# Tying the later modulation's fp32 matmuls together and recording them behind attention scores, in a planned one-core backbone kernel

## The chip, the cores and the metric

The kernel runs on one core of a Trainium2 chip. Its time is that of one execution on the device, in microseconds, the median of several runs. The core has TensorE (PE, the matrix engine; its weight loads are listed apart as PEld), VectorE (DVE), ScalarE (ACT), GpSimd (POOL), and SyncE (SP), whose queue issues most of the transfers between the device's memory and the core's. Every engine carries out its instructions in the order in which the program gives them to it and waits on the others by semaphores.

## The reference

Two layers over 512 latent tokens and 256 context tokens of width 1024, all in fp32. Each layer scales and shifts its normalised input by a modulation computed from a conditioning vector, mixes tokens by attention, gates, projects, and adds the result back. Layer 0 is differential attention with 8 heads, each with two maps of head dimension 64; layer 1 has 8 query heads of dimension 128 on 2 key/value heads.

```python
def adaln(cvec, w, b):
    m = jax.nn.silu(cvec) @ w + b                      # 1024 -> 3 * 1024
    return jnp.split(m, 3, axis=-1)                    # shift, scale, gate

for i in range(DEPTH):
    last = i == DEPTH - 1
    shift, scale, gate = adaln(c, ada_w[i], ada_b[i])
    cshift, cscale, cgate = adaln(c_ctx, ada_w[i], ada_b[i])
    h  = rms_norm(x,  pre_g[i]) * (1.0 + scale)  + shift
    hc = rms_norm(xc, pre_g[i]) * (1.0 + cscale) + cshift
    # layer 0: o1 - lam * o2 of two softmax maps, per-head norm, silu gate, w_out
    # layer 1: grouped queries with normalised q and k, silu gate, w_out
    y, yc = mixer(h, hc, ...)
    x = x + gate * rms_norm(y, post_g[i])
    if not last:
        xc = xc + cgate * rms_norm(yc, post_g[i])
```

## The kernel before

Weights and activations are split into a high and a low fp32r part, and a product is three matmuls (`whi` with `h` high and low, `wlo` with `h`). Projections, scores and the product of probabilities with values (PV) all run on TensorE. In layer 0 a head has six query tiles of 128: four latent ones and two of the context. Its scores (`sc<-qk,qk`) contract over 64 rows, two maps side by side in the two halves of the array: twelve matmuls for a latent query tile, or eighteen where a context tile goes with it. VectorE and ScalarE turn them into probabilities (`sm`, `p`, `pp`), a pair of query tiles shares one `pp`; VectorE transposes it in blocks of 32, SyncE writes it to memory (`dr<-pp`) and reads it back transposed (`at<-dr`, four pieces), ScalarE and VectorE split it into `ah` and `al`, and only then can TensorE do the PV matmuls (`bk<-ah,vhi` and so on).

**The later modulation.** The modulation that the start does not need (layer 0's gate and all of layer 1's, six sections named in `SECS`) is computed during layer 0's heads, in twelve groups, two for a section. `grp_load` reads 1 MB of fp32 weights (`araw`, one buffer). `grp_mm` does four fp32 matmuls of 32 columns of the array each, 512 wide, into the four quarters of one PSUM bank (`bk<-araw,s`); ScalarE copies the first group's bank to `arow`, VectorE adds the second's to it, and the next load starts. `ada1_finish` or `gate0_finish` then turns a section's row into columns (a VectorE transposition, a matmul with `fold`, small VectorE operations).

**What sets the order.** The kernel is first recorded, not built: class `Plan` keeps every operation with its producers, and a list scheduler (`schedule`) walks through it with a price for each operation. For TensorE it has four kinds: M (ordinary matmul), T (transposition), S (scores), A (32-column groups), with extra nanoseconds where the kind changes. It runs twelve passes, keeps the best, and then applies `MOVES`, a list of random seeds each of which shifts the keys of some operations (`shift`). The resulting order of each engine is fixed by `Emit.chain`, and the program is built in it. Ahead of that, `flow` decides in which sequence things are recorded: streams of `Step`s with due times, for layer 0 the scores (`S_`), the splitting of probabilities (`T_`), PV (`M_`), the per-head norm (`X_`) and the modulation groups (`A_`), between which projections of later heads and the output projection are filled in. A step may have a `HOT0` priority; `chained(prev)` makes a matmul follow `prev` with nothing between on TensorE.

In the kernel before, `acc_steps` makes each group and each finish a `Step` of its own in `A_`, without priority; `ACCN` spreads three of them over each of heads 2 to 7. All instructions carry the line of the helper that emits them (501 before, 493 after), so the profile is read by tile names: `araw` is a group, `sc<-qk` are layer 0's scores, `sc<-kh,qh` layer 1's, `raw` a weight load, `whi`/`wlo` its parts.

Of the kernel before, what the change touches and what calls it, by code (L numbers as in the profile page):

```python
# [9 lines left out]
F32 = mybir.dt.float32  # L10
F32R = mybir.dt.float32r
AF = mybir.ActivationFunctionType
ALU = mybir.AluOpType
# [3 lines left out]
P = 128  # L17
# [19 lines left out]
ACCN = (0, 0, 3, 3, 3, 3, 3, 3)  # L37
ACD = 5.0
SUMS = ()
# [50 lines left out]
CTX_AT = {2: 0, 3: 1}  # L90
DRB = 6
# [3 lines left out]
def f32(ap):  # L95
# [6 lines left out]
MOVES = (361629762, 413672696, 596582793, 497724196, 683463327, 110464215, 110999015, 165414765, 369530505, 1059228683,  # L102
# [13 lines left out]
SLACK = 0  # L116


# [22 lines left out]
class Plan:  # L141
# [195 lines left out]
    def schedule(self, rank):  # L337
# [15 lines left out]
        while len(order) < count:  # L353
# [2018 lines left out]
```

## Time and profile before

| | before |
|---|---|
| median of 3 runs | 750.67 us (749.71 to 754.61) |
| the profiled execution | 751.56 us |
| its span, first to last instruction | 749.8 us |
| TensorE busy | 731.8 us (98%) |
| TensorE weight loads | 651.8 us (87%) |
| VectorE, ScalarE, GpSimd busy | 552.5, 482.0, 464.4 us |
| mean granted TensorE clock | 0.997 of full speed |

The span leaves out 1.8 us of the execution, before the first and behind the last instruction. Busy time of TensorE runs to the modelled end of a matmul, and matmuls are pipelined, so one starts before the last has ended: what a matmul takes of the stream is the distance from its start to the next one's. An fp32 matmul of a group is listed as two, so a group shows as x8. A "granted clock" of 0.5 in a stretch means that the engine ran at half speed there.

### The profile page before, as it was taken

To read this page: it belongs to the slowest core of one execution; us is meant where nothing else is said; L and a number is where in the kernel's file an instruction comes from. 1 tells how busy PE (TensorE), PEld (TensorE's weight loads), DVE (VectorE), ACT (ScalarE), POOL (GpSimd) and SP (SyncE) were. 2 spreads that over 40 slices of the span, in tenths; PEclk is the share of its full clock that TensorE was granted. 3 is DMA by queue.
4 is the path that set the end of the run, shared out by engine and by line. 5 is a ranking of instruction groups with operands and counts; after the bars stand their busy time and mean duration, and the time that the engine had idled before them with its cause. 6 is when DMAs were issued, how large, how long until landed. Compare 5 with 4: busy or idle time off the path is not lost.

```text
span 749.8 us, 13955 instructions
## 1 busy us (share of the span) xinstructions
PE 731.8 (98%) x5046; PEld 651.8 (87%) x5046; DVE 552.5 (74%) x874; ACT 482.0 (64%) x1085; POOL 464.4 (62%) x512
## 2 busy tenths in 40 slices
PE   7999999999999999989999999999999999999996
PEld 5789888888888998878989998899999888888986
DVE  5345778989898876788787743899547878888654
ACT  5634567776577666656658843785466777778751
POOL 4545888699496857786744311465898859762501
PEclk9999999999999999999999999999999999999999
DMA  9932347435748775385837352034526786798603
GB/s 353 406 122 101 135 146 208 137 118 197 235 132 225 206 212 169 127 222 191 224 131 208 114 197 85 2 97 137 169 85 190 216 258 209 224 248 254 202 29 112
DMA packets 51444, 131.75 MB, mean 176 GB/s; under 512 B 6448, under 2 KB 27184, under 8 KB 49840
## 3 DMA queue, kind: packets, MB, share of 16 engines
q1 hardware_dynamic: 47952, 125.73, 53.6%
q10 hardware_dynamic: 3424, 5.15, 2.1%
q8 instruction: 39, 0.64, 0.4%
q14 instruction: 29, 0.24, 0.1%
HBM read 97.56 MB, written 29.10 MB: 169 GB/s over the span
## 4 chain that ended last, share of the span: by engine, by line
PE 79%; DMA 9%; DVE 5%; ACT 2%; POOL 2%; issue 2%; SPq 0%; ACTq 0%; DVEq 0%; POOLq 0%
PE bk L501 65%; PE sc L501 14%; DMA at<-dr 3%; DMA dr<-pp 2%; DMA raw<-in_a_w 2%; DVE pp L501 1%; DVE al L501 1%; DMA ag<-in_ada_s 1%; ACT ah L501 1%; DMA xt<-in_x 1%; DMA sw<-qr 0%; POOL pp L501 0%; SPq L501 0%; POOL qr L501 0%; DVE sm L501 0%
## 5 line engine op out<-in xcount | busy, mean ns | idle before, releaser
L501 PE MATMUL bk<-whi,h 128*128 128x256 f32 (+1 forms) x1184 | 242.6, 298 | 0.3 <-ACT g L501 0.2
L501 PE MATMUL bk<-h,whi 128*128 128x512 f32 (+2 forms) x832 | 224.8, 350 | 0.0
L501 POOL TENSOR_TENSOR wlo<-raw,whi 128x256 fp32r<-128x256 f32 x200 | 171.6, 883 | 66.1 <-ACT whi L501 65.9
L501 PEld LDWEIGHTS bk<-whi,h 128*128 128x128 f32 x1184 | 189.4, 188 | 11.5 <-issue 1.7
L501 PE MATMUL bk<-wlo,h 128*128 128x256 f32 (+1 forms) x592 | 173.9, 298 | 0.0
L501 PEld LDWEIGHTS bk<-h,whi 128*128 128x128 f32 x832 | 144.2, 188 | 18.3 <-issue 2.5
L501 PE MATMUL bk<-h,wlo 128*128 128x512 f32 (+2 forms) x416 | 143.1, 349 | 0.0
L501 DVE TENSOR_REDUCE sm<-sc 128x1 f32<-128x768 f32 (+1 forms) x128 | 102.7, 811 | 19.0 <-PE sc L501 13.9
L501 PEld LDWEIGHTS bk<-wlo,h 128*128 128x128 f32 x592 | 110.6, 188 | 4.6 <-POOL wlo L501 0.8
L501 DVE TENSOR_TENSOR al<-at,ah 128x512 fp32r<-128x512 f32 x103 | 93.6, 929 | 22.5 <-ACT ah L501 17.4
L501 POOL TENSOR_SCALAR pp<-pp,sm 128x768 f32<-128x768 f32 (+1 forms) x78 | 79.1, 1017 | 43.1 <-DVE sm L501 42.5
L501 ACT CAST whi<-raw 128x1024 fp32r<-128x1024 f32 (+1 forms) x70 | 71.5, 1022 | 31.4 <-PE bk L501 23.4
L501 PEld LDWEIGHTS bk<-h,wlo 128*128 128x128 f32 x416 | 77.9, 189 | 7.5 <-issue 0.8
L501 ACT CAST ah<-at 128x512 fp32r<-128x512 f32 x103 | 61.6, 617 | 26.6 <-PE bk L501 10.2
L501 DVE STREAM_TRANSPOSE pp<-pp 128x1536 f32<-128x1536 f32 (+1 forms) x39 | 61.2, 1574 | 4.1 <-POOL pp L501 4.0
L501 POOL TENSOR_TENSOR sz<-sz,za 128x384 f32<-128x384 f32 (+1 forms) x24 | 31.0, 1299 | 39.7 <-ACT za L501 38.5
L501 ACT ACTIVATE pp<-sc,sm 128x768 f32<-128x768 f32 (+1 forms) x46 | 35.5, 772 | 25.2 <-DVE sm L501 22.6
L501 PE MATMUL sc<-qk,qk 64*128 64x256 f32 (+1 forms) x480 | 49.5, 343 | 0.0
L501 PEld LDWEIGHTS sc<-qk,qk 64*128 64x128 f32 x480 | 38.1, 189 | 12.3 <-issue 3.1
L501 ACT ACTIVATE jk<-bk 128x128 f32<-128x128 f32 (+4 forms) x66 | 22.8, 346 | 40.1 <-PE bk L501 21.6
L501 DVE SCALAR_TENSOR_TENSOR pp<-p,sm,pp 128x768 f32<-128x768 f32 x32 | 42.0, 1314 | 3.0 <-POOL pp L501 1.6
L501 ACT ACTIVATE za<-za 128x384 f32<-128x384 f32 (+1 forms) x72 | 40.2, 561 | 6.1 <-DVE za L501 5.4
(209 smaller groups left out, 1358.3 us busy)
## 6 DMA issues: line engine op xcount, KB each, us to landing
dr<-pp SPq DMA_DIRECT2D x32, 768.0 KB, 4.2
at<-dr SPq DMA_DIRECT2D x128, 192.0 KB, 4.4
raw<-in_a_w SPq DMA_DIRECT2D x30, 512.0 KB, 4.4
araw<-in_ada_g SPq DMA_DIRECT2D x12, 1024.0 KB, 5.2
raw<-in_b_w SPq DMA_DIRECT2D x20, 512.0 KB, 3.7
ag<-in_ada_s SPq DMA_DIRECT2D x16, 512.0 KB, 9.2
raw<-in_w_out SPq DMA_DIRECT2D x16, 512.0 KB, 4.8
sw<-qr ACTq DMA_DIRECT2D x32, 128.0 KB, 3.1
```

Source lines behind the costliest of these rows:

```text
L501: self.ops.append(getattr(eng, meth)(*args, **kw))
```

## The change

The groups lose their own steps. `GRP_AT` assigns group 0 to query tile 1 of head 2, group 1 to its tile 3, and so on to tile 3 of head 7. The scores step of such a tile calls `grp_mm` right behind its scores matmuls and inside its priority, and is priced 1.0 us more in `flow`. Inside `grp_mm`, matmuls 2 to 4 are chained each to the one ahead; the first has no such tie, since `prev` starts as `None` there. The finish of a section stays a step of `A_`, due after the scores step of its second group. `SUMS` was empty, so taking out its branches changes no instruction. The planner's extra costs at a change of kind are altered, and `MOVES` is a new list of 63 seeds in place of 137. Every engine carries out the same instructions in the same number as before (TensorE 4923 matmuls, VectorE 876, ScalarE 905, GpSimd 517).

```diff
-ACCN = (0, 0, 3, 3, 3, 3, 3, 3)
-SUMS = ()
+GRP_AT = {(h, qt): 2 * i + j for i, h in enumerate(range(2, 8)) for j, qt in enumerate((1, 3))}
-MOVES = (361629762, 413672696, 596582793, 497724196, 683463327, 110464215, 110999015, 165414765, 369530505, 1059228683,
...
+MOVES = (1023873503, 705729452, 956325129, 977087635, 15758088, 1019643688, 934273247, 352177696, 148174306, 445949630,
...
                 k, pen = op.kind, 0
-                if last is not None and k != last and k in "SA":
+                if last in ("M", "T") and k in "SA":
                     pen = 92
...
                 elif k == "A":
-                    gap = 7 if run % 4 != 3 else op.cost * 2 + 103
+                    gap = 7 if run % 4 != 3 else op.cost * 2 + 15
                 else:
-                    gap = op.cost + (60 if late else 57 if last in ("S", "A") else 0)
-                if last == "S" and k != "S" and st == free[e]:
-                    st += 94
+                    gap = op.cost + (106 if last in ("S", "A") else 60 if late else 0)
+                if last in ("S", "A") and k != last and st == free[e]:
+                    st += 88
...
         def grp_mm(i):
             layer, sec, g = groups[i]
-            t = loaded.pop(i)
...
+            t, prev = loaded.pop(i), None
             if g == 0:
...
+            o = trp()
+            for j in range(4):
+                with after(prev), chained(prev):
+                    prev = nc.tensor.matmul(o[32 * j:32 * j + 32, :], s32[:, 4 * g + j, :], t[:, j, :], start=True, stop=True)
+            r = rows[layer, sec]
+            if g == 0:
+                nc.scalar.copy(r, o)
             else:
-                o = trp()
-                prev = None
-                for j in range(4):
-                    with after(prev):
-                        prev = nc.tensor.matmul(o[32 * j:32 * j + 32, :], s32[:, 4 * g + j, :], t[:, j, :], start=True, stop=True)
...
+                nc.vector.tensor_tensor(r, o, r, ALU.add)
             grp_load(i + 1)
...
                 prev = s_mm(sc, h, qt, 512, C, prev)
                 if e is not None:
                     s_mm(sc, h, NQ + e, T, C, prev)
+                if (h, qt) in GRP_AT:
+                    grp_mm(GRP_AT[h, qt])
+                if e is not None:
                     if e == 0:
...
-            return res, [Step(lambda qt=qt: unit(qt), 1.6 if h < KT - 1 and qt in CTX_AT else 1.2) for qt in qts]
+            return res, [Step(lambda qt=qt: unit(qt), 1.2 + 0.4 * (h < KT - 1 and qt in CTX_AT) + 1.0 * ((h, qt) in GRP_AT)) for qt in qts]
...
-        def acc_steps():
-            res = []
-            grp_load(0)
-            for i, (layer, sec, g) in enumerate(groups):
-                res.append(Step(lambda i=i: grp_mm(i), 0.2 if groups[i][:2] in SUMS else 1.5, hot=False))
...
+        def grp_end(i, step):
+            layer, sec, _ = groups[i]
+            f = (lambda: gate0_finish(sec - 4)) if layer == 0 else (lambda: ada1_finish(layer, sec))
+            return Step(f, 2.0 if layer == 0 else 1.0, [(step, ACD)], hot=False)
...
-            lo, hi = sum(ACCN[:h]), sum(ACCN[:h + 1])
-            for i in range(lo, min(hi, len(A_))):
-                A_[i].at = at_ + per * (i - lo + 0.5) / (hi - lo)
...
+                for st_, qt in zip(u, (2 * ch, 2 * ch + 1)):
+                    if GRP_AT.get((h, qt), 0) % 2:
+                        A_.append(grp_end(GRP_AT[h, qt], st_))
```

How the order moves is shown at three places.

TensorE at the second group (`araw`, four matmuls). Before, it stands among projections:

```order
L501 MATMUL bk_71<-whi_1763,h_641 128x256
L501 MATMUL bk_71<-wlo_1764,h_641 128x256
L501 MATMUL bk_71<-whi_1763,h_642 128x256
L501 MATMUL bk_72<-araw_1862,s_134 32x512 x4
L501 MATMUL bk_70<-h_287,whi_2205 128x512
L501 MATMUL bk_73<-h_287,whi_1970 128x256
L501 MATMUL bk_73<-h_288,whi_1970 128x256
```

After, it stands earlier in the program, among PV matmuls of head 1 (`ah`, `al`); the scores that it is recorded behind (tile 3 of head 2) follow only 27 rows later:

```order
L493 MATMUL bk_72<-whi_1653,h_382 128x256
L493 MATMUL bk_71<-al_1695,vhi_799 128x256 x2
L493 MATMUL bk_71<-ah_1717,vhi_799 128x256 x2
L493 MATMUL bk_71<-ah_1717,vlo_800 128x256 x2
L493 MATMUL bk_73<-araw_1834,s_134 32x512 x4
L493 MATMUL bk_71<-al_1718,vhi_799 128x256 x2
L493 MATMUL bk_70<-ah_1793,vhi_799 128x256 x2
```

The second group still has no scores next to it. The fourth group (recorded behind tile 3 of head 3) has them after the change: it stands ahead of scores of head 4:

```order
L493 MATMUL bk_71<-h_382,whi_2324 128x512
L493 MATMUL bk_71<-h_383,whi_2324 128x512
L493 MATMUL bk_71<-h_382,wlo_2325 128x512
L493 MATMUL bk_72<-araw_2530,s_134 32x512 x4
L493 MATMUL sc_75<-qk_2736,qk_2734 128x512
L493 MATMUL sc_74<-qk_2736,qk_2734 128x512
L493 MATMUL sc_75<-qk_2737,qk_2734 128x512
```

Behind it start twelve scores matmuls (`sc<-qk`), with no projection between.

VectorE at the second pair of query tiles of head 5 of layer 0: `sm` are row maxima and sums, `al` the low parts of transposed probabilities, `pp` this pair's probabilities, `arow` the modulation row. Before:

```order
L501 TENSOR_REDUCE sm_3760<-sc_75 128x1
L501 TENSOR_REDUCE sm_3752<-sc_74 128x1
L501 TENSOR_TENSOR al_3693<-at_3586,ah_3692 128x512
L501 TENSOR_TENSOR al_3709<-at_3586,ah_3708 128x512
L501 TENSOR_REDUCE sm_3760<-sc_75 128x1
L501 RECIPROCAL sm_3732<-sm_3732 128x2 x2
L501 TENSOR_TENSOR arow_3601<-bk_71,arow_3601 128x512
L501 TENSOR_TENSOR sm_3732<-sm_3732,nlam 128x2
L501 STREAM_TRANSPOSE arow_3601<-arow_3601 128x512
L501 SCALAR_TENSOR_TENSOR pp_3657<-p_3751,sm_3732,pp_3657 128x24x32
L501 SCALAR_TENSOR_TENSOR pp_3655<-at_3656,sm_3732,pp_3655 128x8x32
L501 STREAM_TRANSPOSE pp_3657<-pp_3657 128x1536
```

After:

```order
L493 TENSOR_REDUCE sm_3802<-sc_75 128x1
L493 TENSOR_REDUCE sm_3794<-sc_74 128x1
L493 TENSOR_TENSOR sw_3575<-sw_3575,rope 128x512
L493 TENSOR_TENSOR arow_3603<-bk_73,arow_3603 128x512
L493 TENSOR_REDUCE sm_3802<-sc_75 128x1
L493 RECIPROCAL sm_3767<-sm_3767 128x2
L493 STREAM_TRANSPOSE arow_3603<-arow_3603 128x512
L493 RECIPROCAL sm_3767<-sm_3767 128x2
L493 TENSOR_TENSOR al_3747<-at_3624,ah_3746 128x512
L493 TENSOR_TENSOR sm_3767<-sm_3767,nlam 128x2
L493 SCALAR_TENSOR_TENSOR pp_3708<-p_3793,sm_3767,pp_3708 128x24x32
L493 SCALAR_TENSOR_TENSOR pp_3706<-at_3707,sm_3767,pp_3706 128x8x32
```

One of the two `al` that stood ahead of the addition to `arow` is gone from there (it stands nine rows ahead of it now); the addition and the transposition of `arow` come ahead of the second reciprocal, and the other `al` behind it.

SyncE's queue in layer 1, heads 4 and 5: `dr` is a pair's probabilities on the way to memory, `at` its transposed reads (four pieces), `raw` weight loads. Before:

```order
L501 DMA raw_7931<-in_post_g 128x512
L501 DMA raw_8038<-in_b_w 128x1024
L501 DMA dr_7912<-pp_7836 128x1536
L501 DMA at_7911<-dr_7912 32x4x384
L501 DMA dr_8011<-pp_7977 128x1536
L501 DMA at_7911<-dr_7912 32x4x384 x3
L501 DMA raw_8214<-in_w_out 128x1024
L501 DMA raw_8334<-in_w_out 128x1024
L501 DMA at_8010<-dr_8011 32x4x384 x4
```

After:

```order
L493 DMA raw_7931<-in_post_g 128x512
L493 DMA at_7761<-dr_7762 32x4x384 x4
L493 DMA dr_7912<-pp_7836 128x1536
L493 DMA at_7911<-dr_7912 32x4x384 x4
L493 DMA dr_8011<-pp_7977 128x1536
L493 DMA raw_8038<-in_b_w 128x1024
L493 DMA raw_8214<-in_w_out 128x1024
L493 DMA at_8010<-dr_8011 32x4x384 x4
```

The load `raw_8038` moves behind the reads of the pair `dr_7912`, which are no longer split by the next `dr`; `raw_8334` moves behind the reads of the next pair.

## Rows read from the trace of the kernel before

**Rows 1.** The page, busy time, share of the span and instructions of each engine.

```profile
PE 731.8 (98%) x5046; PEld 651.8 (87%) x5046; DVE 552.5 (74%) x874; ACT 482.0 (64%) x1085; POOL 464.4 (62%) x512
```

**Rows 2.** Timeline of TensorE between projections: start us, us, engine, line, operation, tiles.

```profile
146.20 0.40 PE L501 MATMUL bk<-h,whi 128*128 128x256 f32 x2
146.44 0.28 PE L501 MATMUL bk<-h,wlo 128*128 128x256 f32 x1
146.65 1.06 PE L501 MATMUL bk<-araw,s 128*32 128x512 f32 x8
147.64 0.62 PE L501 MATMUL bk<-h,whi 128*128 128x384 f32 x2
...
148.27 0.51 PE L501 MATMUL bk<-h,whi 128*128 128x384 f32 x2
```

**Rows 3.** Timeline of TensorE, a group behind scores.

```profile
222.14 1.32 PE L501 MATMUL sc<-qk,qk 64*128 64x512 f32 x12
223.39 1.06 PE L501 MATMUL bk<-araw,s 128*32 128x512 f32 x8
```

**Rows 4.** Timeline of TensorE, a group ahead of scores.

```profile
267.41 1.07 PE L501 MATMUL bk<-araw,s 128*32 128x512 f32 x8
268.40 1.32 PE L501 MATMUL sc<-qk,qk 64*128 64x512 f32 x12
269.65 0.44 PE L501 MATMUL bk<-sqs,ones_r 128*128 128x384 f32 x1
```

**Rows 5.** Timeline of TensorE, head 5; in brackets idle time and releaser.

```profile
335.03 0.28 PE L501 MATMUL bk<-h,whi 128*128 128x256 f32 x1
337.57 0.50 PE L501 MATMUL bk<-ah,vhi 128*128 128x256 f32 x2 [2.26 <-ACT ah L501]
```

**Rows 6.** Windows behind it: us, busy time by engine, PEclk, DMA share, GB/s.

```profile
338.45:341.86 3.41, 3.41 (x21) 2.89 (x21) 1.73 (x4) 2.69 (x6) 0.64 (x1) 0.50 0.79 320
```

**Rows 7.** Chain that ended last, within 300 to 345: start us, us, what.

```profile
307.59 1.60 PE sc L501 x16
...
319.16 4.25 DVE pp L501 x3
...
323.43 3.32 DMA dr<-pp
...
326.76 5.61 DMA at<-dr
...
332.44 4.45 DMA raw<-in_a_w
```

**Rows 8.** Timeline of VectorE, ahead of head 5's probabilities.

```profile
312.45 2.83 DVE L501 TENSOR_TENSOR al<-at,ah 128x512 fp32r<-128x512 f32 x2
...
316.77 0.69 DVE L501 TENSOR_TENSOR arow<-bk,arow 128x512 f32<-128x512 f32 x1 [0.35 <-PE bk L501]
```

**Rows 9.** Timeline of SyncE's queue, end of layer 0.

```profile
405.48 2.68 SPq L501 DMA_DIRECT2D at<-dr  x4
408.27 0.36 SPq L501 DMA_DIRECT2D raw<-in_w_out  x1
```

**Rows 10.** Timeline of TensorE, first use of what those reads bring.

```profile
419.39 0.39 PE L501 MATMUL bk<-ah,vhi 128*128 128x256 f32 x2
```

**Rows 11.** Windows, heads of layer 1, columns as in rows 6.

```profile
600.00:700.00 100.00, 96.68 (x608) 87.45 (x607) 83.94 (x121) 77.81 (x169) 63.16 (x65) 1.00 0.80 235
```

**Rows 12.** Timeline of SyncE's queue, the first weights.

```profile
5.08 1.30 SPq L501 DMA_DIRECT2D raw<-in_a_w  x2
```

**Rows 13.** Timeline of TensorE, the first projection.

```profile
17.99 0.72 PE L501 MATMUL sc<-h,whi 128*128 128x512 f32 x2 [0.66 <-ACT h L501]
```

**Rows 14.** Windows, the start.

```profile
0.00:40.00 40.00, 34.15 (x260) 26.70 (x261) 17.19 (x44) 23.98 (x43) 22.22 (x40) 1.00 0.96 368
```

**Rows 15.** Timeline of TensorE, layer 1, head 5, second pair: scores, PV.

```profile
648.03 0.34 PE L501 MATMUL sc<-kh,ql 128*128 128x384 f32 x1
...
678.23 0.40 PE L501 MATMUL bk<-ah,vh 128*128 128x256 f32 x2
```

More of the change, by code (lines that the diff above doesn't have):

```diff
@@ L1292, in grp_mm @@
             layer, sec, g = groups[i]
-            t = loaded.pop(i)
-            on_dve = (layer, sec) in SUMS
+            t, prev = loaded.pop(i), None
             if g == 0:
-                rows[layer, sec] = [t0.tile([P, 512], F32, tag=f"arow{v}", name=nm("arow"), bufs=1) for v in range(1 + on_dve)]
-            if on_dve:
-                for j in range(4):
-                    for v, r in enumerate(rows[layer, sec]):
-                        s = scol[:, v, 4 * g + j:4 * g + j + 1]
-                        if g + j == 0:
-                            nc.vector.tensor_scalar(r, t[:, j, :], s, None, ALU.mult)
-                        else:
-                            nc.vector.scalar_tensor_tensor(r, t[:, j, :], s, r, ALU.mult, ALU.add)
-            else:
-                o = trp()
-                prev = None
-                for j in range(4):
-                    with after(prev):
-                        prev = nc.tensor.matmul(o[32 * j:32 * j + 32, :], s32[:, 4 * g + j, :], t[:, j, :], start=True, stop=True)
-                r, = rows[layer, sec]
-                if g == 0:
-                    nc.scalar.copy(r, o)
-                else:
-                    nc.vector.tensor_tensor(r, o, r, ALU.add)
+                rows[layer, sec] = t0.tile([P, 512], F32, tag="arow", name=nm("arow"), bufs=1)
+            o = trp()
[5 more added lines that the diff above has]
+                nc.scalar.copy(r, o)
+            else:
+                nc.vector.tensor_tensor(r, o, r, ALU.add)
             grp_load(i + 1)
@@ L1320, in ada1_finish @@
             o = trp()
-            if (layer, sec) in SUMS:
-                for b in range(8):
-                    v, k = divmod(b, 4)
-                    nc.tensor.matmul(o[:, b:b + 1], r[v][:, k * P:(k + 1) * P], ones[:, :1], start=b == 0, stop=b == 7)
-                ov_ = o[:, :8].rearrange("p (v k) -> p v k", v=2)
-            else:
-                r, = r
-                nc.vector.transpose(r, r)
-                nc.tensor.matmul(
-                    o[:, :32], fold.rearrange("p q c -> p (q c)"),
-                    r.rearrange("p (b x) -> p b x", x=32)[:, :, 0:2], start=True, stop=True)
-                fo = t0.tile([P, 2, 4, 4], F32, tag="fo", name=nm("fo"), bufs=1)
-                nc.vector.tensor_tensor(
-                    fo, o[:, :32].rearrange("p (k q v) -> p v k q", k=4, q=4),
-                    quad.rearrange("p (a b q) -> p a b q", a=1, b=1).to_broadcast([P, 2, 4, 4]), ALU.mult)
-                fc = t0.tile([P, 2, 4], F32, tag="fc", name=nm("fc"), bufs=1)
-                nc.vector.tensor_reduce(fc, fo, AX.X, ALU.add)
-                ov_ = fc
-            mod_cols(layer, sec % 2, sec // 2, lambda v: ov_[:, v, :])
+            nc.vector.transpose(r, r)
+            nc.tensor.matmul(
+                o[:, :32], fold.rearrange("p q c -> p (q c)"),
+                r.rearrange("p (b x) -> p b x", x=32)[:, :, 0:2], start=True, stop=True)
+            fo = t0.tile([P, 2, 4, 4], F32, tag="fo", name=nm("fo"), bufs=1)
+            nc.vector.tensor_tensor(
+                fo, o[:, :32].rearrange("p (k q v) -> p v k q", k=4, q=4),
+                quad.rearrange("p (a b q) -> p a b q", a=1, b=1).to_broadcast([P, 2, 4, 4]), ALU.mult)
+            fc = t0.tile([P, 2, 4], F32, tag="fc", name=nm("fc"), bufs=1)
+            nc.vector.tensor_reduce(fc, fo, AX.X, ALU.add)
+            mod_cols(layer, sec % 2, sec // 2, lambda v: fc[:, v, :])
         qk, pend, qk_t = {}, {}, {}
@@ L1629, in gate0_finish @@
         def gate0_finish(half):
-            r, = rows.pop((0, 4 + half))
+            r = rows.pop((0, 4 + half))
             hi, lo = (t0.tile([P, 512], F32R, tag="tmp", name=nm("rs"), bufs=3) for _ in range(2))
@@ L1671, in tile_backbone @@
             add({"qk": qk_proj, "v": v_proj, "z": z_proj}[kind](i))
[L1672 to L1683 removed]
+        def grp_end(i, step):
+            layer, sec, _ = groups[i]
+            f = (lambda: gate0_finish(sec - 4)) if layer == 0 else (lambda: ada1_finish(layer, sec))
+            return Step(f, 2.0 if layer == 0 else 1.0, [(step, ACD)], hot=False)
+        grp_load(0)
+        S_, T_, M_, X_, A_ = [], [], [], [], []
         at_ = clock[0] + FZ
@@ L1765, in tile_backbone @@
             at_ += per
-        for st_ in A_[sum(ACCN):]:
-            st_.at = at_
         add(out_early())
```

6 lines of the change are left out of this document (removed), and 19 rows, old and new, of the table MOVES.

## The prediction, made before the changed kernel was run

> **What bounds the kernel.** First the busy times: TensorE works 731.8 of the 749.8 us span [rows 1]; TensorE's own stream is the time, plus the places where it stands still or switches its mode. So I read TensorE's timeline next, at the groups that the change moves. There the reader is to compare starts, since matmuls overlap. Two 256-wide matmuls take 0.24 us to the next start (146.20 to 146.44), 0.12 each, but a group starts 0.21 after the one ahead of it (146.44 to 146.65): 0.09 more. It holds TensorE 0.99 us (to 147.64). The two 384-wide matmuls behind it last 0.62 where two later ones last 0.51: 0.11 more [rows 2]. Beside scores: twelve scores take 1.25 us to the next start whether a group follows (222.14 to 223.39) [rows 3] or an ordinary matmul (268.40 to 269.65), and a group gives over to scores in the same 0.99 as to a matmul (267.41 to 268.40) [rows 4]. So a group that touches scores is spared 0.09 + 0.11 = 0.20 us, and no more.
>
> Then the pauses. The largest is in head 5 of the differential layer: TensorE stands still for 2.26 us ahead of 337.57, waiting for `ah` of that head's second pair of query tiles [rows 5]. Behind it the granted clock is 0.50, the lower of the two levels (1.2 GHz), for 3.41 us [rows 6]; half of that, 1.7 us, is lost. Together 4.0 us. The chain of waits says what led there: the scores end at 309.2 (307.59 + 1.60), VectorE finishes the probabilities from 319.16 to 323.4, they go to memory in 3.32 us, come back transposed from 326.76 on, and the last piece on the queue ends at 336.9 [rows 7]. The other pauses lie in layer 1: between 600 and 700 us TensorE works 96.68 of 100 us, at full clock [rows 11].
>
> The sum is made on the profiled execution, 751.56 us, which is 0.89 above the median of the runs, 750.67.
>
> **The change, part by part.**
>
> *Groups and chaining.* Only matmuls 2 to 4 of a group are tied to the first; the first is not tied to the scores, it is merely recorded behind them and has their priority, and the planner may even set it ahead of them. The order shows what comes of it: before, four groups of twelve touch scores, after it five (three ahead of scores, two behind). The four matmuls of a group stood together before too, so tying them buys nothing. Along TensorE's whole order there are 48 entries into runs of scores or groups before, 46 after. An entry with its exit costs 0.09 + 0.20 = 0.29: the exit is the 0.11 behind it and 0.09 that I take by likeness to the entry (it lies within the 0.99 and the 1.25, and no row parts it off; without it the term is −0.3). A contact of scores and group costs 0.09. Before 48 × 0.29 + 4 × 0.09 = 14.28, after 46 × 0.29 + 5 × 0.09 = 13.79: **−0.5 us**.
>
> The Trainium skill, "TensorEngine Tiling (Array Packing)", Key Properties, has: "Changing tiling mode (not just tile) drains the TensorE". That speaks against putting groups beside scores, for scores take half the rows and a group's matmuls a quarter of the columns, which is a change of mode again. The trace agrees in part, as a group behind scores starts no sooner than an ordinary matmul. By the rule, contacts would save nothing and the term would be the two missing entries, −0.6, the same within a tenth.
>
> *New prices and seeds of the planner.* They move nearly every row on every engine, while the instructions stay the same in number; so only places count that were late or become late.
>
> *Head 5.* Before, VectorE does two `al` (2.83 us from 312.45) and the `arow` addition, which itself waited 0.35 us for TensorE, ahead of the pair's `pp` work [rows 8]. After, one of the two `al` stands nine rows earlier, and the addition further ahead, for a group that TensorE issues earlier. Half of 2.83 plus 0.35 is 1.8 us off the chain at best, nothing at worst (if the moved `al` only delays what follows it). TensorE's cover, the rows between those scores and their first PV matmul at the trace's slots, is 26.0 us before and 26.3 after. So 0.3 to 2.1 off the stall; I take 1.3, near the middle, leaving 1.0. Pauses of at most that length in layer 1 were followed by a full clock [rows 11], so I count 0.7 of the clock's 1.7 as saved too. **−2.0 us**, bounds 0 and −4.0.
>
> The Trainium skill, "TensorE: Matmul & The Clock Gate", Terms, puts the penalty at the throttled time × (1 − K/N). With K/N at one half and the 3.41 us this is the 1.7 us that the row gave; the trace agrees.
>
> *End of layer 0.* The last group moves behind the last full score unit, so its addition (0.69 us at 316.77 [rows 8]) and a transposition of about that length fall among VectorE's last `al`. On SP's queue a weight load (`raw_697`) now stands ahead of the transposed reads of head 7's last pair; before it followed them, at 408.27, the reads having begun at 405.48 [rows 9]. It can hold the reads up by 2.8 us; they are first used at 419.39 [rows 10], so that stays covered. **+0.4**, bounds 0 and +1.5 (both operations late).
>
> *Start.* SP now issues four more modulation loads of 512 KB ahead of the first weights, which left at 5.08 us [rows 12] and served a projection at 17.99 that ACT's `h` released [rows 13]. At the 368 GB/s of that stretch [rows 14] 2.1 MB are 5.7 us. The weights had 12.9 us from issue to use and keep 7.2; in a crowded queue I put them up to 1.5 us late. TensorE does modulation matmuls in the meantime that it did later. **+0.3**, bounds −0.5 (only that) and +1.5.
>
> *Layer 1.* In heads 4 to 6 TensorE's cover of three pairs falls from 28 to 30 us to 24 to 26, while SP no longer splits one pair's reads or puts that weight load ahead of them. The first lengthens pauses, the second shortens them; **0**, bounds −3 (all that is lost there) and +8 (next part).
>
> Sum: −0.5 − 2.0 + 0.4 + 0.3 = −1.8: 749.8 on the profiled execution's scale, **748.9 us** as a median.
>
> **Rivals.**
>
> *The pauses go.* If the moved `al` is all gained and the clock stays up, head 5 gives −4.0: with −0.5, a median of 746.2. If half to all of layer 1's 3.3 us goes as well, 744.5 to 742.9. For it: VectorE did wait ahead of that `arow`. Against: the rest of the chain, memory both ways, is untouched. Chance 0.22.
>
> *Layer 1 becomes late*, the other sign. Place: pairs of heads 4 to 6. The second pair of head 5 had its last scores at 648.03 and its first PV matmul at 678.23 without idle before it [rows 15], 29.9 us from the scores' end. In the new order TensorE has 24.9 us of work in between. If the way through softmax, memory and back keeps its length, TensorE waits up to 5.0 us there, and up to 3 more for the neighbours. It decides if the transposed probabilities land later than about 24 us after their scores. For it: the count, and that the other pairs of this layer already leave pauses. Against: a straighter queue, and a way that was this long because nobody needed it sooner. +3 to +8 with the other terms gives 752 to 757. Chance 0.24, a third of it past 758, where a fall of the clock as in rows 6 comes on top.
>
> *The change does what its words say*, all twelve groups behind scores: eight more contacts, −1.6 where one more gives −0.2. The order excludes it: 0.02, with whatever else is unforeseen.
>
> **Numbers.** Forecast (pauses traded, 746.5 to 752) 0.52, pauses gone 0.22, layer 1 late 0.24, other 0.02. What a measurement here can tell from no change is about 1%, 7.5 us: below 743.2 or above 758.2. Faster by more: 0.09, the far end of the case with pauses gone. Slower by more: 0.08. The same: 0.83. The range leaves out those far ends and the last microsecond of the late case: **743.5 to 756**.
>
> **What would show it.** Right: a pause of about 1 us or less ahead of `ah` near 337, and a granted clock near 1.00 for most of 335 to 345; 0.21 us still ahead of a group between projections; about 3 us lost between 600 and 700. Wrong towards faster: no pause at head 5 and under 2 us lost in layer 1. Wrong towards slower: pauses of 2 us or more ahead of `ah` in layer 1's heads 4 to 6, or between 400 and 425, or a first projection past 19.5 us.

## The result, and the profile after

The changed kernel takes 752.03 us (median of 21 runs, 750.27 to 755.35), the kernel before 749.52 (21 runs, 747.16 to 754.61): a ratio of 1.0031, 95% interval [1.0018, 1.0045]. The forecast was 748.9 us, 0.2% faster; it is 0.3% slower, by some 2.4 us: inside the range of 743.5 to 756, but moved the other way. Two more measurements of the same kernel gave 1.0017 [0.9996, 1.0039] and 1.0036 [1.0020, 1.0053].

The profiled execution of the change, though, took 750.27 us, less than the profiled one of before (751.56). So the two profiles by themselves point the other way from the runs. That is the puzzle of this case. On the profiles' scale the change moved by −1.3 us, near the −1.8 of the sum, but that is luck: two further profiled executions of the same kernel took 752.61 and 752.13 us. Where head 5 had its pause [rows 5], the changed kernel has none, and the clock stays up [rows 6]. TensorE's timeline there:

```profile
335.83 0.28 PE L493 MATMUL bk<-h,wlo 128*128 128x256 f32 x1
335.95 0.40 PE L493 MATMUL bk<-ah,vhi 128*128 128x256 f32 x2
```

and the windows (us, busy time of PE, PEld, DVE, ACT, POOL, then PEclk, DMA share, GB/s), with those of layer 1's heads [rows 11]:

```profile
335.00:340.00 5.00, 5.00 (x36) 4.62 (x35) 5.00 (x5) 1.78 (x4) 3.02 (x2) 1.00 0.16 60
340.00:345.00 5.00, 5.00 (x37) 3.62 (x37) 5.00 (x7) 4.46 (x13) 1.97 (x3) 1.00 0.24 59
600.00:700.00 100.00, 95.96 (x606) 86.72 (x605) 85.25 (x116) 79.45 (x172) 65.01 (x66) 1.00 0.76 226
```

VectorE's part of that chain (compare [rows 7, 8]) has a longer wait for the group now, 0.83 us. But the addition and the transposition of `arow` now stand ahead of the second reciprocal, where VectorE waited 0.56 us before, and one `al` is gone; so `pp` begins at 316.88, before at 319.16. First the wait of before, then the rows of after:

```profile
316.26 0.17 DVE L501 RECIPROCAL sm<-sm 128x2 f32<-128x2 f32 x1 [0.56 <-ACT at L501]
```

```profile
313.66 0.69 DVE L493 TENSOR_TENSOR arow<-bk,arow 128x512 f32<-128x512 f32 x1 [0.83 <-PE bk L493]
...
314.67 0.69 DVE L493 STREAM_TRANSPOSE arow<-arow 128x512 f32<-128x512 f32 x1
...
315.40 0.67 DVE L493 TENSOR_TENSOR al<-at,ah 128x512 fp32r<-128x512 f32 x1
...
316.88 1.15 DVE L493 SCALAR_TENSOR_TENSOR pp<-p,sm,pp 128x768 f32<-128x768 f32 x1
```

A group between ordinary matmuls still pays on entry and exit (compare [rows 2]): 0.32 us from two 256-wide matmuls to the group (two slots of 0.12 and 0.08 more), and 0.34 behind it for two that take 0.23 further on. A group ahead of scores pays on entry, 0.33 us, and hands over in the same 1.00 us (compare [rows 4]).

```profile
160.60 0.39 PE L493 MATMUL bk<-ah,vlo 128*128 128x256 f32 x2
160.92 1.06 PE L493 MATMUL bk<-araw,s 128*32 128x512 f32 x8
161.92 0.50 PE L493 MATMUL bk<-al,vhi 128*128 128x256 f32 x2
162.26 0.40 PE L493 MATMUL bk<-ah,vhi 128*128 128x256 f32 x2
162.49 0.40 PE L493 MATMUL bk<-ah,vlo 128*128 128x256 f32 x2
```

```profile
143.75 0.40 PE L493 MATMUL bk<-h,whi 128*128 128x256 f32 x2
144.08 1.07 PE L493 MATMUL bk<-araw,s 128*32 128x512 f32 x8
145.08 1.32 PE L493 MATMUL sc<-qk,qk 64*128 64x512 f32 x12
```

What looks worse is at the start and in head 3. At the start the first projection runs at 19.08 us, before at 17.99 [rows 13], and a later one waits for `wlo`:

```profile
16.73 0.61 PE L493 MATMUL bk<-sel,row 128*128 128x2 f32 x4 [0.52 <-ACT row L493]
...
19.08 1.26 PE L493 MATMUL sc<-h,whi 128*128 128x512 f32 x4 [0.74 <-ACT whi L493]
...
22.96 0.38 PE L493 MATMUL bk<-wlo,h 128*128 128x256 f32 x1 [0.42 <-POOL wlo L493]
```

The wait of the first projection, at 19.08, ends with ScalarE's two casts of its weights, which ScalarE did at 12.40 before and does at 18.42 now:

```profile
12.40 1.13 ACT L501 CAST whi<-raw 128x512 fp32r<-128x512 f32 x2
```

```profile
18.42 1.12 ACT L493 CAST whi<-raw 128x512 fp32r<-128x512 f32 x2
```

TensorE's busy time between 15 and 25 us fell from 9.22 to 8.33 (the windows of before, then of after):

```profile
15.00:25.00 10.00, 9.22 (x76) 5.05 (x66) 3.19 (x9) 4.51 (x8) 3.14 (x6) 1.00 1.03 408
```

```profile
15.00:25.00 10.00, 8.33 (x61) 4.72 (x50) 2.87 (x8) 4.73 (x9) 5.87 (x8) 1.00 1.03 406
```

In head 3, TensorE waits for one `al` at 238.42 for 1.01 us. VectorE does it behind the per-head norm's product `gT` and a transposition, and while GpSimd works too it takes 1.97 us:

```profile
237.02 0.39 PE L493 MATMUL bk<-ah,vlo 128*128 128x256 f32 x2
238.42 0.51 PE L493 MATMUL bk<-al,vhi 128*128 128x256 f32 x2 [1.01 <-DVE al L493]
```

```profile
234.07 1.77 DVE L493 SCALAR_TENSOR_TENSOR gT<-gT,subg,sq 128x768 f32<-128x768 f32 x1
235.77 0.70 DVE L493 STREAM_TRANSPOSE pp<-pp 128x512 f32<-128x512 f32 x1
236.40 1.97 DVE L493 TENSOR_TENSOR al<-at,ah 128x512 fp32r<-128x512 f32 x1
```

To compare executions by equal work I cut at two places where both orders have finished exactly the same operations: TensorE's 460th matmul (some 80 us) and its 2992nd (some 447 us). From the first transposition on, in us:

| profiled execution | start, to the 460th | heads, to the 2992nd | rest | fall of the clock at |
|---|---|---|---|---|
| before | 73.17 | 366.80 | 301.75 | 338 |
| before, second profile | 73.10 | 367.57 | 301.99 | 338 |
| changed | 73.71 | 364.63 | 301.85 | none |
| changed, second | 73.74 | 364.81 | 304.15 | 628 |
| changed, third | 74.38 | 363.76 | 304.30 | 19 |

(the drop to half clock at each kernel's very end, when TensorE has finished, is left out).

### The profile page after: what moved, and what is told of

The parts are those of the page before. It is cut to its first block, busy times and chain, and to the rows that moved or that the text cites. A ratio compares the mean times of both kernels' runs of the same rounds, so it can differ in the third digit from the quotient of the medians.

```text
span 748.2 us, 13977 instructions
## 1 busy us (share of the span) xinstructions
PE 730.4 (98%) x5046; PEld 651.6 (87%) x5046; DVE 550.1 (74%) x874; ACT 480.1 (64%) x1085; POOL 464.1 (62%) x512
## 4 chain that ended last, share of the span: by engine, by line
PE 76%; DMA 10%; DVE 5%; ACT 3%; issue 3%; POOL 3%; SPq 1%; ACTq 0%; DVEq 0%; POOLq 0%
PE bk L493 63%; PE sc L493 13%; DMA sw<-qr 2%; DMA dr<-pp 2%; DMA at<-dr 2%; DVE pp L493 2%; DMA raw<-in_a_w 1%; DVE al L493 1%; DMA xt<-in_x 1%; DVE sm L493 1%; DMA raw<-in_b_w 1%; POOL qr L493 1%; POOL qk L493 1%; ACT pp L493 1%; POOL wlo L493 1%
## 5 line engine op out<-in xcount | busy, mean ns | idle before, releaser
L493 PE MATMUL bk<-h,whi 128*128 128x512 f32 (+2 forms) x832 | 221.7, 348 | 0.0
L493 POOL TENSOR_TENSOR wlo<-raw,whi 128x256 fp32r<-128x256 f32 x200 | 167.3, 862 | 51.9 <-ACT whi L493 51.9
L493 POOL TENSOR_SCALAR pp<-pp,sm 128x768 f32<-128x768 f32 (+1 forms) x78 | 80.6, 1037 | 49.6 <-DVE sm L493 45.6
L493 POOL TENSOR_TENSOR sz<-sz,za 128x384 f32<-128x384 f32 (+1 forms) x24 | 29.8, 1243 | 29.9 <-ACT za L493 29.5
```

The source lines that it names most:

```text
L493: self.ops.append(getattr(eng, meth)(*args, **kw))
```

## The experiments

All orders below are edits of the finished plan: single operations or whole stretches are set in another place, and nothing is computed otherwise. `FIRST` is the first 712 operations in the order of the other kernel, `LAST` the last 3000.

**The changed kernel once more.** No edit.

> The changed kernel once more, for a second profile and its ratio beside the next three on one chip. All theories: 1.002 to 1.0045 of before, as measured so far (1.0031). Theory heads (a pause in the heads of layer 0, with a fall of the clock behind it, that comes in some executions and not in others): this profile shows a pause of 2 us or more between 100 and 425 us, or a clock below 0.9 in some 5 us of that stretch. Theories start and layer 1: it shows none, as the first profile of it.

Ratio 1.0017 [0.9996, 1.0039]. No pause over 1.1 us between 100 and 425, which speaks against the theory of the heads, but the clock fell at 628 us, in layer 1 (the table's second changed row). A profile of this kernel is one of several possible executions.

**The start, and layer 1, of before: three hybrids.**

```diff
-        return self.schedule(lambda o: (key[o], o.n))
+        return self.splice(self.schedule(lambda o: (key[o], o.n)))
+    def splice(self, order):
+        mine, turn = set(OTHER), {e: iter([n for n in OTHER if self.ops[n].eng == e]) for e in SELF}
+        return [self.ops[next(turn[o.eng])] if o.n in mine else o for o in order]
+OTHER = (...)     # operations 0 to 588, or 4354 on, or both, in the order of before
```

> The changed kernel, but every engine does the start (the first 589 recorded operations, up to some 70 us) in the order of the kernel before. Theory start: the first scores come 1.4 us sooner (at 71.4 in place of 72.7), the rest follows, ratio to before 1.001. Theory layer 1 and theory heads: the pauses behind the start take the gain up, ratio 1.002 to 1.0035.

> The changed kernel, but every engine does what is recorded behind layer 0's heads (operations 4354 on, from some 425 us) in the order of the kernel before. Theory layer 1: the 2 us that the changed kernel loses between the first scores of layer 1 and its end come back, ratio to before 1.000 to 1.001. Theory start and theory heads: 1.002 to 1.0035.

> The changed kernel with both: start and layer 1 in the order of before, so that only layer 0's heads, with the groups behind scores, are those of the change. Theory heads: nothing comes back, 1.002 to 1.004. Theories start and layer 1, alone or together: 0.997 to 1.001, the groups themselves being worth half a microsecond at most.

Ratios 1.0016 [0.9999, 1.0034], 1.0015 [0.9999, 1.0031], 1.0009 [0.9992, 1.0026]: all between the kernels, none apart from another. The first and third have a seam: their first projection came at 17.9 as in before, but TensorE then stood 0.9 us ahead of 65.3, where ScalarE's `vhi` and VectorE's `vlo` of one order met TensorE's banks of the other. Inconclusive; the later runs cut where the orders agree.

**A second profile of before.** No edit.

> The kernel before, for a second profile. Theory one-off (the pause of head 5 with the fall of the clock behind it belonged to that one execution, which at 751.6 us was 2 us over the median): no half clock between 300 and 425 us, the pause there under 1.5 us, the stretch from the 460th to the 2992nd matmul 362.5 to 364 us in place of 366.8. Theory standing (the pause comes in every execution): 365.5 us or more in that stretch, a pause over 2 us.

The pause and the half clock were there again, so "one-off" fell (though a third profile, under "The mirror", does not have them):

```profile
335.59 0.28 PE L501 MATMUL bk<-h,whi 128*128 128x256 f32 x1
338.12 0.80 PE L501 MATMUL bk<-ah,vhi 128*128 128x256 f32 x2 [2.25 <-ACT ah L501]
```

```profile
337.73:341.15 3.42, 3.03 (x14) 2.81 (x16) 2.64 (x5) 2.82 (x7) 0.00 (x0) 0.50 0.77 248
```

But this execution took 752.32 us, 3.4 over the median of the runs beside it (748.95), and the first profiled one 2.0 over its own. The profiled executions of the changed kernel lay 1.8 under, 2.0 over and 0.4 over theirs. Nothing on record makes a profiled execution another kind of run: each execution of these experiments comes with its span and its mean clock, and the profiled one is among those that the median is taken of.

**Head 5's pause taken out of before.** The decisive run for the term of −2.0.

```diff
+        order.remove(self.ops[3167])                              # arow's addition
+        order.insert(order.index(self.ops[3153]), self.ops[3167])  # behind pp's large transposition
+        order.remove(self.ops[3270])                              # arow's transposition
+        order.insert(order.index(self.ops[3153]), self.ops[3270])
```

> The kernel before with two VectorE operations moved: the addition to arow and its transposition, which stand ahead of head 5's probabilities, go behind their large transposition. Both theories expect the same of the profile: the chain 1.7 us shorter, the pause at 335 to 337 down from 2.4 to about 0.7, no half clock behind it, the stretch from the 460th to the 2992nd matmul 363.3 in place of 366.8 and 367.6. They part on the ordinary runs. Theory profiled only (head 5's pause and the fall of the clock are far smaller in runs without the profiler, which explains why both profiled executions of before stand 2.0 to 3.4 us over their medians): ratio 0.999 to 1.0005. Theory standing (they come in every run): 0.994 to 0.996.

The profile lost the pause and the fall (TensorE 10.00 of 10 us at full clock), and its heads took 364.78 us in place of 366.80 and 367.57:

```profile
330.00:340.00 10.00, 10.00 (x80) 7.97 (x77) 8.53 (x18) 6.96 (x14) 6.77 (x6) 1.00 1.03 266
```

The ordinary runs did not move: 749.45 us, ratio 0.9999 [0.9981, 1.0017]. Four microseconds would be 0.9947 and the two of my sum 0.9973; the interval excludes both, and allows a gain of 1.4 us at most. The profile itself shows where the gain went: its heads are 2.0 and 2.8 us shorter than those of the two profiles of before, but its rest took 303.63 us in place of 301.75 and 301.99, with a fall of the clock in layer 1 that those two do not have:

```profile
626.80:630.20 3.40, 3.40 (x15) 3.40 (x16) 2.66 (x5) 2.35 (x7) 3.40 (x4) 0.50 0.46 153
```

So this execution, at 751.09 us, stands 1.6 over its median without the pause, and "profiled only" is not shown: an execution over its median need not owe that to the pause. Nor do all executions of before have a fall. The results list the mean clock of 147 further ones, taken beside these runs: 72 show 0.998 or more, which among the twenty profiles of this case only executions without a fall ahead of TensorE's end reach. Their median is 748.95 us, that of the 65 at 0.996 or less 750.38. In 41 executions of the changed kernel the same two groups have 751.74 and 751.76: its loss stands without a fall too, so falls of the clock do not make it.

**`al` ahead of `gT`; the start without a seam; both.**

```diff
+        order.remove(self.ops[2269])
+        order.insert(order.index(self.ops[2061]), self.ops[2269])       # al_first
+        order = [self.ops[n] for n in FIRST] + [o for o in order if o.n not in FIRST]   # clean_start
```

> The changed kernel with one VectorE operation moved: the low part al that TensorE awaits at 237 us ahead of the per-head norm's product gT, which stands two operations ahead of it. Theory pause (the 1.0 to 1.2 us at 237, seen in all five profiles with the changed heads, are lost in full): the pause is gone, the stretch from the 460th to the 2992nd matmul 1 us shorter (363.6), ratio to before 1.001. Theory taken up (a later wait takes its place): the stretch stays at 364.4 to 364.8.

> The changed kernel, all engines in the order of before for the first 712 operations (up to some 80 us, where the two orders have done the same operations, so that no seam is left). Theory start: 73.2 us from the first transposition to the 460th matmul in place of 73.7, 0.5 us of the whole. Rival: the transfers bound the start, so it stays 73.7.

> Both edits: the start of before and al ahead of gT. Theories start and pause together: 1.5 us under the changed kernel, ratio to before 0.999 to 1.001. If the loss lies elsewhere: 1.002 or more.

1.0024 [1.0004, 1.0043], 1.0006 [0.9987, 1.0025], 1.0003 [0.9986, 1.0020]. The wait is gone in both runs with the edit, but another one opens (0.81 us at 243.84 in the first, 1.01 at 242.38 in the other, for VectorE's `gate`). The heads' stretch was 363.88 and 363.83 us with `al` ahead of `gT`, and 364.4 to 365.5 in the first two changed profiles and the three hybrids without it; but profiles below without the edit took 363.56 (`table_heads`) to 366.05 (`table_tail`), so the stretch does not part the edit from chance. Nor do the ordinary runs: `clean_start` and `both`, which differ by it alone and ran on one chip, have medians of 749.82 and 749.80 us. The start was 73.00 us with the old order (73.35 with both edits), as expected.

**The mirror: before with the change's start.**

```diff
+        order = [self.ops[n] for n in FIRST] + [o for o in order if o.n not in FIRST]
```

> The kernel before with the changed kernel's order for the first 712 operations (no seam: the same operations are done by then in both). Theory start: 73.7 us from the first transposition to the 460th matmul in place of 73.1, or 74.4 with half clock in it, and a ratio of 1.0008 to 1.002. If the start costs nothing in ordinary runs: 0.999 to 1.0005.

The stretch came out as the start theory had it, 73.74 us, but the ratio was 1.0000 [0.9978, 1.0022]: what I had expected if the start costs nothing, with an interval that reaches over the 1.0008 to 1.002 of the theory.

This run says something on head 5 too. Its heads have the order of before, untouched, and yet the pause ahead of `ah` was 0.47 us and the clock stayed up (its only fall ahead of TensorE's end came at 627):

```profile
337.00 0.28 PE L504 MATMUL bk<-h,whi 128*128 128x256 f32 x1
337.75 0.50 PE L504 MATMUL bk<-ah,vhi 128*128 128x256 f32 x2 [0.47 <-ACT ah L504]
```

```profile
335.00:345.00 10.00, 9.53 (x81) 7.42 (x79) 8.38 (x14) 7.44 (x16) 6.15 (x6) 1.00 0.74 207
```

So the pause does not stand in every execution of that order; whether the later start took it away or chance was not tried.

**Three more groups beside scores.**

```diff
+        for n, to in ((1680, 1662), (2074, 2381), (3011, 3148)):
+            grp = self.ops[n:n + 4]
+            order = [o for o in order if o not in grp]
+            at = order.index(self.ops[to])
+            order[at:at] = grp
```

> The changed kernel with three more groups brought into contact with scores (the 2nd, the 3rd and the 7th, each moved directly ahead of the next run of scores; eight of twelve then touch). My price of 0.20 us a contact: the gaps at changes of mode come to 0.6 us less in the profile, and the time falls by as much, ratio to before 1.0015 to 1.0025. Rival, the rule that every change of mode drains and a contact saves nothing: the gaps stay as they are.

760.60 us, ratio 1.0153 [1.0126, 1.0180]: over 9 us above what was expected, and neither theory had it. The other engines kept their order. ScalarE stands 6.18 us in front of its copy of the moved 7th group, and the exponentials that free the scores' banks queue behind that copy, so the scores next to the group wait 2.54 us; the clock halves behind it, and once more after a like wait (2.10 us for ScalarE's `p`) at 185:

```profile
312.18 0.58 ACT L499 COPY arow<-bk 128x512 f32<-128x512 f32 x1 [6.18 <-PE bk L499]
```

```profile
311.05 1.06 PE L499 MATMUL bk<-araw,s 128*32 128x512 f32 x8
314.66 1.65 PE L499 MATMUL sc<-qk,qk 64*128 64x512 f32 x6 [2.54 <-ACT at L499]
```

```profile
314.68:318.09 3.41, 3.41 (x20) 2.90 (x21) 2.16 (x5) 2.12 (x5) 1.00 (x1) 0.50 0.97 398
```

The groups with an undisturbed neighbour still hand over in 1.00 us. Without the idle time, the starts at changes of mode come to 27.0 us in place of 27.3: less, against the rival, but half of the 0.6 that I expected of three contacts. The run's time says nothing on that price.

**A table of two by two.** Start of before (`FIRST`) and last 3000 operations of before (`LAST`), with the change's heads, all on one chip.

```diff
+        order = [self.ops[n] for n in FIRST] + [o for o in order if o.n not in FIRST]
+        order = [o for o in order if o.n not in LAST] + [self.ops[n] for n in LAST]
```

> The changed kernel (start, heads and layer 1 of the change). All theories: 1.002 to 1.003 of before.

> The changed kernel with the start of before (first 712 operations). Theory start (four loads ahead of the weights delay the first projections by 0.6 us, and a clock that falls among the start's pauses in some runs adds to it): 0.0013 to 0.0020 under the changed kernel in this and the next comparison of starts. Theory layer 1: as the changed kernel.

> The changed kernel with the last 3000 operations (from some 450 us: the rest of the projections of layer 1, its attention and its output) in the order of before. Theory layer 1 (its pauses between 600 and 630 us are longer by the new order, or the clock falls oftener behind them): 0.0010 to 0.0020 under the changed kernel. Theory start: as the changed kernel, within 0.0007.

> Start and last 3000 operations of before, only the heads of the change between, with the groups recorded behind scores. Theories start and layer 1, either: 0.999 to 1.0005 of before, the change's heads being worth the half microsecond of fewer changes of mode. Theory heads (VectorE's pause at 237 us and what else the new order does there): 1.001 to 1.002.

| | start of the change | start of before |
|---|---|---|
| rest of the change | 1.0036 [1.0020, 1.0053] | 1.0010 [0.9994, 1.0025] |
| rest of before | 1.0017 [1.0002, 1.0032] | 1.0009 [0.9994, 1.0024] |

The start: 0.0026 and 0.0008, on the mean 0.0017, 1.3 us, which the cells' intervals (half-widths of some 0.0015) hardly part from nothing. The last 3000: 0.0019 and 0.0001, on the mean 0.0010, which they don't part from it. The heads alone: 1.0009, not parted from 1 either. The profiles show how the start can cost more than the 0.5 us of its stretch. In both with the start of the change (`table_change` and `table_tail`) the clock fell there; the first of them:

```profile
18.72 0.79 PE L493 MATMUL sc<-h,whi 128*128 128x512 f32 x1 [0.74 <-ACT whi L493]
```

```profile
18.58:21.99 3.41, 3.27 (x8) 2.59 (x9) 0.58 (x1) 1.66 (x3) 3.24 (x5) 0.50 1.02 408
```

Of the ten profiles with the change's start and a clean join, four had this fall (`al_first`, `table_change`, `table_tail`, and `sp_of_before` of the next section, which has SyncE's queue otherwise), and their stretch was 74.4 to 74.5 us, that of the others 73.7 and once 74.0. Of the ten with the start of before none had it. So in the profiles the start costs some 0.6 us, and 0.7 more where the clock falls.

**Which part of the start.**

```diff
+        order = [self.ops[next(turn)] if o.n in QUEUE_FIRST else o for o in order]   # SyncE as before
+        for cast in (126, 123):                                                    # casts_early only
+            order.remove(self.ops[cast])
+            order.insert(order.index(self.ops[100]), self.ops[cast])
```

> The changed kernel with SyncE's queue alone in the order of before for the start: the weights are loaded ahead of the four modulation loads again. Theory casts (ScalarE does the two casts of these weights only behind both activations of h, at 18.4 us, so that an earlier load helps nobody): the first projection stays at 19.0 to 19.1, 73.7 or more from the first transposition to the 460th matmul, ratio 1.002 to 1.004 as the changed kernel. Theory loads: first projection at 18.0 to 18.4, 73.1 to 73.3, ratio 1.001 to 1.002.

> The same, and ScalarE's two casts of the first weights ahead of the third copy of the transposed input, where the kernel before has them. Both theories: the first projection no later than 18.4, the stretch 73.0 to 73.3, no half clock between 15 and 25 us, ratio 1.0005 to 1.002. If the start's loss lies in TensorE's own new order instead: 73.7, and the half clock still comes.

1.0023 [1.0006, 1.0040] and 1.0019 [1.0005, 1.0033]; the stretch 74.49 (with a fall of the clock) and 74.03. With the loads alone restored nothing comes back: the casts still stand behind both activations. With the casts restored too, the first projection runs 0.24 us sooner, at 18.84, behind a modulation group that now waits for its own load; and the next wait is for the weights behind, whose cast ends at 22.5:

```profile
17.84 1.07 PE L499 MATMUL bk<-ag,s 128*32 128x512 f32 x8 [0.26 <-DMA ag<-in_ada_s]
18.84 1.19 PE L499 MATMUL sc<-h,whi 128*128 128x512 f32 x4
...
22.54 0.50 PE L499 MATMUL bk<-whi,h 128*128 128x256 f32 x2 [0.66 <-ACT whi L499]
```

```profile
21.45 1.04 ACT L499 CAST whi<-raw 128x1024 fp32r<-128x1024 f32 x1 [2.68 <-DMA raw<-in_a_w]
```

Both theories missed: setting back the loads alone, or loads and casts, does not bring the start's loss back. That does not clear them, since with the restored queue other work waits for its loads. TensorE's own order there (it takes both modulation rows and a further group ahead of any projection, where before it took a projection between them) was not tried by itself, so the cause of the start's loss stays open.

**The best pieces together.** `FIRST` and `LAST` of before, the heads of the change, `al` ahead of `gT`.

```diff
+        order = [self.ops[n] for n in FIRST] + [o for o in order if o.n not in FIRST]
+        order = [o for o in order if o.n not in LAST] + [self.ops[n] for n in LAST]
+        order.remove(self.ops[2269])
+        order.insert(order.index(self.ops[2061]), self.ops[2269])
```

> Start and last 3000 operations of before, the heads of the change, and al ahead of gT (the pause at 237). The sum of the parts: 0.9990 to 1.0005 of before. If it is under 0.9990, the regrouping of the heads is worth something by itself; at 1.001, the heads of the change are no better than those of before.

748.85 us against 749.86, ratio 0.9984 [0.9969, 0.9998]: faster than the kernel before, with an interval that just clears 1 (one interval of eighteen here), and faster than the changed one (1.0031). It lies under the sum of the parts that I expected. So nothing shows the heads of the change to be a loss. The moved `al` is not what shows in it: the heads' stretch was 363.72 us, that of `table_heads`, which differs by this edit alone, 363.56.

## Why the prediction was wrong, point by point

*Head 5, −2.0 us: the step that failed.* The term took 1.3 us of a pause and 0.7 of a fall of the clock, both read from one profile, as standing in every execution of before, and as gained for good where they go. The pause itself went, as forecast and further: none of the sixteen profiles with the change's heads has a pause over 0.4 us or a half clock near 338. But neither assumption held. The pause was 0.47 us at full clock in a third profile with before's heads (`before_late_start`), and about half of the executions of before have no fall ahead of TensorE's end. Taking the event out of before on purpose (`arow_late`) gave 0.9999 [0.9981, 1.0017], which excludes the −2.0; in its profile the heads gained 2.0 to 2.8 us and the rest lost 1.6 to 1.9, with the fall in layer 1 in place of head 5. That 0.7 of the fall would be saved rested on pauses of about 1 us in layer 1 behind which the clock stayed up; in nine of twenty profiles it fell right behind them. So the term is nothing within 1.4 us, a bound that I had written down (0) and not weighed. I had one profile, 0.89 us over the median of three runs; the median of 21 puts it at 2.0 over. Without the term the sum is +0.2, a kernel as fast as before or slower. Nearly all the signs that I had named for "right" came in the first profile, and the runs went the other way: they were signs of one execution.

*Start, +0.3: right sign, too small.* Profiles: 0.55 us in the stretch, some 0.7 more where the clock falls; table: 1.3 us, inside the bounds (−0.5 to +1.5), while the mirror run gave 0.0. My mechanism, weights late behind four loads, is not shown to be the whole of it: the casts and TensorE's own order moved with the loads, and setting back loads and casts did not bring the time back.

*Groups, −0.5: the sum came out, its place did not.* The starts at changes of mode, added up from matmul to next start, come to 29.4 us before and 28.8 after. But the difference lies in the start's own modulation groups (`ag`), which TensorE enters five times in place of six, and in idle time: for the later groups and the scores alone, and without idle time, the sum is 23.7 us in both. So the groups that the change moves gained nothing that shows. The four matmuls of a group take the same 0.996 us in both kernels. What the words of the change say (groups behind scores) did not happen, as the order had shown.

*End of layer 0, +0.4: too much.* The changed profile lists no wait of TensorE between 385 and 430 us.

*Layer 1, 0 with −3 and +8: not parted from 0.* It lost 4.0 of 100 us in the changed profile, 3.3 before. The rest from the 2992nd matmul on took 301.8 us in the first profiles of both, but 304.2 and 304.3 in the two later ones of the changed kernel and 302.0 in the second of before. The table's 0.0010 for it is inside the noise. The rival that set the slower end did not come: the second pair of head 5 had its last scores at 647.40 and its first PV matmul at 672.78, 25.0 us apart, with the 24.9 us of cover that I counted and no wait (0.35 to 0.55 us in three of the other ten profiles with this order):

```profile
647.40 0.42 PE L493 MATMUL sc<-kh,ql 128*128 128x384 f32 x1
...
672.78 0.40 PE L493 MATMUL bk<-ah,vh 128*128 128x256 f32 x2
```

So the 29.9 us of before [rows 15] are not what the way needs, which is the argument that I held against this rival; whether the straighter queue shortened it too was not tried.

*Not foreseen:* the wait for `al` in head 3, 0.7 to 1.0 us in every profile of the change's heads as they stand. I had looked for places that were late before, and this one was not. That it costs time is not shown, since another wait opens where it is taken away.

*What stays open.* 2.4 us are to be told. The table gives the start 1.3, the mirror run (1.0000) nothing, though its interval allows 1.0022. Some 0.2 us lie outside the span of instructions, which leaves out 2.0 us in the median execution of the changed kernel and 1.8 before (1.8 too in the five runs of the changed kernel that have layer 1 in the order of before). The rest, and how much of it is layer 1 or the `al` of head 3, is below what these runs can part.

## What to carry to other kernels

A pause with a halved clock behind it is the most tempting row of a profile and the least safe one to charge. Before it enters a sum, profile the same order more than once: an event that is missing from one of the profiles belongs in the range, at its cost, and not in the sum. Then take it out on purpose and compare the medians of many runs, since a fall of the clock that goes at one place can come at another. A planner that is searched anew redraws the start too, where every transfer is crowded; a shift of half a microsecond there can take the clock with it. And an operation that is moved on one engine must bring its consumers' places on the other engines' queues along, or their in-order queues stop work that has nothing to do with it (some 9 us here over the changed kernel).

## What the runs showed of the hardware

The granted clock fell from 2.4 to 1.2 GHz behind waits that are short beside a matmul stream of 750 us: behind one of 2.25 us (at 338 in both profiles of before), behind 2.10 and 2.54 (at 185 and 315 with eight groups in contact), and at the start around two of 0.5 and 0.7, there in three of eight executions of the same order. In layer 1 it fell between 625 and 636 us in nine of the twenty profiles, with either order of that part, though all twenty have the same two waits there (1.0 to 1.3 us for `al` and 0.46 behind it). The falls shown here lasted 3.41 us at half clock, so one lost up to 1.7 us. So the same order of instructions has more than one time.

An `al` of the same size takes 0.67 us on VectorE at 315.40 and 1.97 at 236.40. GpSimd works beside both; at 236.40 it runs a product of two tensors, at 315.40 an operation of one:

```profile
235.99 1.83 POOL L493 TENSOR_TENSOR gT<-gT,sz 128x768 f32<-128x768 f32 x1 [0.96 <-DVE gT L493]
...
315.32 1.90 POOL L493 TENSOR_SCALAR pp<-pp,sm 128x768 f32<-128x768 f32 x2
```

The Trainium skill, "GPSIMD Engine Reference" (Key points), says that GpSimd's way to the SBUF is shared with VectorE and is contended for when VectorE's instruction has two SBUF inputs, as `al` has. The trace agrees for one kind of GpSimd operation only. Of the 103 such `al` in the changed profile, 40 have GpSimd's product of two tensors beside them for over half of their time, and a median of 1.21 us (0.66 to 2.34); the 20 beside its operation of one tensor have 0.69, and the 33 with GpSimd idle 0.68 (0.65 to 0.69).
